# Eleven of block 2's 22 MLP pairs by seven half-size products, on two sets of banks, with TensorE in written order

## The chip, the cores and the metric

The kernel runs on one NeuronCore of a Trainium2 chip. Its engines work beside each other, each through its own queue of instructions in a fixed order: TensorE (PE, matrix products, with its weight loads shown as PEld), VectorE (DVE), ScalarE (ACT), GpSimd (POOL) and SyncE (SP, which starts the transfers). TensorE writes into PSUM banks, from which VectorE and ScalarE read. The metric is the time of one execution on the device in microseconds. "Columns" are the width of a product's right-hand side: 512 are a whole one, 256 a half one.

## The reference

Two transformer blocks, 512 tokens of width 1024, all in fp32. The change is in the MLP of the second block alone:

```python
u = rmsnorm_2(x, norm_ffn_w[l])
up, gate = jnp.split(u @ w_ffn_up[l], 2, axis=-1)      # 1024 x 5632; D_FF_2 = 2816 = 22 * 128
a = causal_dwconv_2(up, ffn_conv_w[l], ffn_conv_b[l])  # 3 taps over the tokens
x = x + (jax.nn.silu(a) * gate) @ w_ffn_down[l]
...
return rmsnorm_2(x, norm_final_w)
```

## The kernel before

**Products.** An fp32 product is made of three products of numbers split into a high and a low half (mm3, L461 to L463: high by high, high by low, low by high). Activations lie transposed, 128 channels by 512 tokens to a tile; hs is the list of split results of the MLP's pairs.

**Weights.** All weights come in one stream, in the order of weight_order(), as units of 512 KB (eight 128 by 128 blocks). prefetch loads a unit into one of four "raw" buffers, ScalarE casts it to the high half (whi, L258), VectorE subtracts for the low half (wlo, L260); there are five buffers each of whi and wlo. A cast into a whi buffer must wait until TensorE has made the last product with what was in it.

**Block 2's MLP.** The 22 column tiles of up, each with its column tile of gate, are the 22 pairs. hidden2(i) makes a pair: two times 8 x 3 products of 512 columns into one bank each, then its tail of small operations: zp = up times the norm's factor rb (VectorE, L1676), conv3 (a scaling on ScalarE, L1585, two taps on VectorE, L1587), silu (ScalarE, L1678), times gate (VectorE, L1679), split into halves (ScalarE L529, VectorE L530). They run as pairs 0 to 8, eight "downs" (24 products each with w_ffn_down, L1691), pairs 9 to 16, eight downs, pairs 17 to 21. The last six tiles of down stand in a "tail" that goes through the 512 tokens in two halves, with the final norm of each half: sums of squares by small products with ones (L1757, L1759).

**Pairs by seven.** Block 1's MLP (about 400 to 720 us) makes 14 of its 16 pairs another way, with pairg: the pair is taken as a 2 x 2 block matrix of weights times a 2 x 2 block matrix of activations (two k tiles by two token halves, four times), and by a scheme of Strassen's kind this takes seven half-size products in place of eight: 7 x 4 x 3 = 84 of 256 columns in place of 48 of 512. It needs sums of weight blocks (seven_steps: the sums s75, s6, s4 on VectorE, L297, L315, L318; the casts and low halves of three sets of 1024 columns and of the 512 columns of operand "b", L305 and L310) and sums of activation blocks (rights). The seven results collect in four banks. A copy c0 of the first (ScalarE, L380) and four additions on VectorE (L386 to L389) put them together in a tile q that holds up and gate.

**Banks.** There are two kinds, "mm" and "sm", of four each. A plain product takes the next "mm" bank in turn; an "mm" seven pair takes all four. The first bank of a seven pair is free for the next product once c0 is copied.

**Order.** defer(n, f) runs f after n more products have been written; the list scheduler then settles the order of each engine, but block 1's seven pairs run as written on TensorE.

Of the kernel before, what the change touches and what calls it, by code (L numbers as in the profile page):

```python
# [9 lines left out]
F32 = mybir.dt.float32  # L10
F32R = mybir.dt.float32r
I32 = mybir.dt.int32
U8 = mybir.dt.uint8
AF = mybir.ActivationFunctionType
ALU = mybir.AluOpType
# [3 lines left out]
T = 512  # L19
# [40 lines left out]
def weight_order():  # L60


    seq = []
    seven = set()

    def pair(name, n1, n2):
        assert len(seq) % 8 == 0
        seven.add(len(seq) // 8)
        for n, o in ((n1, 0), (n2, 1), (n1, 1), (n2, 0)):
            for k in range(o, 8, 2):  # L70
                seq.append((name, k, n))

    def cols(name, ns, ks):
        for n in ns:
            for k in ks:
                seq.append((name, k, n))

    def rows(name, ks, ns):
        for k in ks:
            for n in ns:  # L80
                seq.append((name, k, n))

    r8 = range(8)
    for lo in (12, 8, 16):
        cols("w_in", range(lo, lo + 4), r8)
    rows("w_in", r8, range(4, 8))
    cols("w_in", range(0, 4), r8)
    cols("w_in", range(20, 24), r8)
    cols("xa_wk", r8, r8)
    rows("xa_wv", r8, range(4))  # L90
    rows("xa_wv", r8, range(4, 8))
    cols("w_out", range(NWO), range(4))
    cols("w_out", range(NWO), range(4, 8))
    cols("w_out", range(NWO, 8), r8)
    cols("xa_wq", r8, r8)
    cols("xa_wo", range(4), range(6))
    cols("xa_wo", range(4), (6, 7))
    cols("xa_wo", range(4, 8), r8)
    for what, i, g in ffn_order():
        if what == 1 and i < NPLAIN:  # L100
            cols("ffn_w1", (2 * i, 2 * i + 1), r8)
        elif what == 1:
            pair("ffn_w1", 2 * i, 2 * i + 1)
        else:
            cols("ffn_w2", [i], range(8 * g, 8 * g + 8))

    cols("w_in_2", [28, 29, 24, 25, 26, 27], r8)
    for i in range(8):
        cols("w_in_2", [8 + i, 16 + i, i], r8)
    cols("w_in_2", [30], r8)  # L110
    cols("w_conv_out_2", r8, r8)
    cols("w_in_2", range(31, 38), r8)
    for i in range(8):
        cols("w_in_2", [38 + i], r8)
        cols("w_attn_out_2", [i], range(4))
    cols("w_mix_out_2", r8, r8)
    for g, (a, b) in enumerate(GROUPS2):
        for i in range(a + (1 if g else 0), b + (1 if b < 22 else 0)):
            cols("w_ffn_up_2", [i, 22 + i], r8)
        cols("w_ffn_down_2", r8, range(a, b))  # L120
    return seq, seven


def ffn_order():


    for i in range(4):
        yield 1, i, 0
    for g in range(4):
        for n in range(8):  # L130
            if g < 3 and n % 4 == 0:
                yield 1, 4 * g + 4 + n // 4, g + 1
            yield 2, n, g
        if g < 3:
            yield 1, 4 * g + 6, g + 1
            yield 1, 4 * g + 7, g + 1


GROUPS2 = [(0, 8), (8, 16), (16, 22)]


# [27 lines left out]
def _build(ctx, tc, nc, A, out, stage):  # L169
# [5 lines left out]
    V, S, G, PE = nc.vector, nc.scalar, nc.gpsimd, nc.tensor  # L175
    cnt = [0]

    def nm(s):
        cnt[0] += 1
        return f"{s}_{cnt[0]}"  # L180

    def t2(dt=F32, shape=(P, T)):
        return ap_.tile(list(shape), dt, tag="t2", bufs=NSLOT, name=nm("t2"))
# [36 lines left out]
    def col(name, i=0, n=1):  # L220
        o = COFF[name][0] + i
        return colt[:, o:o + n]
# [169 lines left out]
    def rights(x, gname, xs):  # L392


        H = T // 2
        f = lambda hl, j: (hl[0][:, j * H:(j + 1) * H], hl[1][:, j * H:(j + 1) * H])
        res = [{} for _ in range(len(xs) // 2)]
        steps = []

        def one(p):  # L400
            st = {}

            def s0():
                st["a"], st["b"] = t2(), t2()
                S.activation(st["a"], x[2 * p], AF.Copy, scale=col(gname, 2 * p))
                S.activation(st["b"], x[2 * p + 1], AF.Copy, scale=col(gname, 2 * p + 1))

            def s1():
                a, b = st["a"], st["b"]
                st["v"], st["w"] = v, w = t2(), t2()  # L410
                V.tensor_sub(v[:, H:], b[:, H:], a[:, H:])
                V.scalar_tensor_tensor(out=w[:, :H], in0=a[:, H:], scalar=1.0, in1=a[:, :H],
                                       op0=ALU.mult, op1=ALU.subtract)
                V.tensor_scalar_mul(v[:, :H], w[:, :H], -1.0)
                V.tensor_sub(w[:, :H], w[:, :H], b[:, H:])
                V.scalar_tensor_tensor(out=w[:, H:], in0=w[:, :H], scalar=-1.0, in1=b[:, :H],
                                       op0=ALU.mult, op1=ALU.subtract)

            def s2():
                vs = split(st["v"])  # L420
                ws = split(st["w"])
                res[p].update({"B11": f(xs[2 * p], 0), "B21": f(xs[2 * p + 1], 0), "B22": f(xs[2 * p + 1], 1),
                               "V1": f(vs, 0), "V7": f(vs, 1), "V6": f(ws, 0), "T4": f(ws, 1)})

            return [s0, s1, s2]

        for p in range(len(xs) // 2):
            steps.extend(one(p))
        return res, steps
# [3 lines left out]
    def defer(n, fn):  # L433

        late.append((wst["i"] + n, fn))
        late.sort(key=lambda e: e[0])
# [37 lines left out]
    def lin(name, n, ks, mv, ps=None, start=True, stop=True, off=0):  # L474
        if ps is None:
            ps = bank()
        for _ in ling(name, n, ks, mv, ps, start, stop, off):
            pass
        return ps
# [41 lines left out]
    def split(src, g=None, shape=(P, T)):  # L521

        hi, lo = t2(F32R, shape), t2(F32R, shape)
        split_to(hi, lo, src, g)
        return hi, lo
# [10 lines left out]
    def zpad():  # L536
        zp = ap_.tile([P, T + 4], F32, tag="t2", bufs=NSLOT, name=nm("zp"))
        G.memset(zp[:, 0:4], 0.0)
        return zp
# [71 lines left out]
    def wide_later(acc, eps, rbt, at, square):  # L611

        def part():
            hi, lo = split(acc)
            ps = bank("sm")
            PE.matmul(ps, lhsT=ones_r, rhs=hi, start=True, stop=False)
            PE.matmul(ps, lhsT=ones_r, rhs=lo, start=False, stop=True)
            if square:
                V.tensor_scalar(rbt, ps, 1.0 / D, eps, op0=ALU.mult, op1=ALU.add)
                V.reciprocal(rbt, rbt)  # L620
                return
            a = tmp()
            V.tensor_scalar(a, ps, 1.0 / D, eps, op0=ALU.mult, op1=ALU.add)
            step(rsqrt_g(rbt, a))

        def step(g):
            if next(g, None) is not None:
                defer(1, lambda: step(g))

        defer(at, part)  # L630

    def acc_tile():
        return ap_.tile([P, T], F32, tag="t2", bufs=NSLOT, name=nm("acc"))


    xs = []
# [4 lines left out]
    acc = acc_tile()  # L641
# [11 lines left out]
    rb = row_bc(rc, 4)  # L653
# [22 lines left out]
    kf, qf, vf, gv, gu, gate, ys = [], [], [], [], [], [], []  # L676
# [530 lines left out]
    acc = acc_tile()  # L1207
# [9 lines left out]
    xs = xs2  # L1217
# [77 lines left out]
    acc = acc_tile()  # L1295
# [8 lines left out]
    xs = xs2  # L1304
# [4 lines left out]
    rops, steps = rights(x, "norm_ffn", xs)  # L1309
# [68 lines left out]
    acc = acc_tile()  # L1378
# [23 lines left out]
    xs = xs2  # L1402

    rc12, rc, rb, rb1 = tinyc(8), tinyc(4), acc_tile(), acc_tile()
# [178 lines left out]
    def conv3(zp, wname, j):  # L1583
        c = tmp()
        S.activation(c, zp[:, 2:2 + T], AF.Copy, scale=col(wname, 3 * j))  # L1585
        for i in (1, 2):
            V.scalar_tensor_tensor(out=c, in0=zp[:, 2 + i:2 + i + T], scalar=col(wname, 3 * j + i),  # L1587
                                   in1=c, op0=ALU.mult, op1=ALU.add)
        return c
# [67 lines left out]
    acc = acc_tile()  # L1657
# [8 lines left out]
    xs = xs2  # L1666


    rb = acc_tile()
    wide_later(acc, 1e-5, rb, 3, False)  # L1670

    def hidden2(i):
        ps = lin("w_ffn_up_2", i, range(8), xs)
        psg = lin("w_ffn_up_2", 22 + i, range(8), xs)
        zp = zpad()
        V.tensor_mul(zp[:, 4:], ps, rb)  # L1676
        c = conv3(zp, "ffn_conv_w_2", i)
        S.activation(c, c, AF.Silu, bias=col("ffn_conv_b_2", i))  # L1678
        V.tensor_mul(c, c, psg)  # L1679
        return split(c)  # L1680

    hs = []
    for g, (a, b) in enumerate(GROUPS2):
        hs += [hidden2(i) for i in range(a + (1 if g else 0), b)]
# [10 lines left out]

    a, b = GROUPS2[2]
    nk = b - a
# [25 lines left out]
    for hf in range(2):  # L1723
        ts = slice(hf * H, (hf + 1) * H)
        acc = acc_tile()
        pss = [None] * 8
        ss = bank("sm")[:, :H]
        st = {}
# [140 lines left out]
```

## Time and profile before

| what | value |
|---|---|
| three runs | 1543.88, 1544.42 and 1546.13 us (median 1544.42) |
| profiled execution | 1543.86 us, its span 1542.1 us |
| mean granted TensorE clock | 0.997 |
| busy share of the span | PE 98%, DVE 65%, ACT 44%, POOL 9% |
| block 2's MLP without its tail | 1159 to 1493 us |

The span runs from the first to the last recorded instruction; some 1.8 us lie outside. Busy shares are means over stages with different limits. PE's busy time comes from modelled ends of pipelined products, so the start-to-start time of products is the better measure of what one costs.

### The profile page before, as it was taken

The numbers are of one execution on the slowest core, as the hardware profiler recorded it, in microseconds if no ns is written. First come the engines' busy times: TensorE is split into PE (matmuls) and PEld (weight loads), VectorE is DVE, ScalarE is ACT, GpSimd is POOL, SyncE is SP. The second block draws the span as 40 slices with busy tenths as digits, with TensorE's granted clock in tenths as the row PEclk, the third lists the DMA queues.
The fourth block names the chain that finished last, engine by engine and source line by source line (L and its number), as shares of the span: only waits on it lengthen the run. The fifth ranks groups of instructions, "written<-read, shape, count | busy, mean of one in ns | idle before, by whom it ended". The sixth has DMA issues, their size and how long they took to land.

```text
span 1542.1 us, 20324 instructions
## 1 busy us (share of the span) xinstructions
PE 1514.8 (98%) x7904; PEld 1274.9 (83%) x7904; DVE 999.0 (65%) x1623; ACT 674.9 (44%) x1117; POOL 143.5 (9%) x162
## 2 busy tenths in 40 slices
PE   8999999999999999999999999999999999999996
PEld 6888898888888888989888888888888888888886
DVE  6897675554786786767688767335546555555557
ACT  6666555443564353535444444333334331332233
POOL 0002120200201212011400000000020002001101
PEclk9999999999999999999999999999999999999998
DMA  6033335221223323324043222222232222232311
GB/s 254 20 111 100 112 130 197 96 68 55 82 72 106 96 95 109 104 83 137 14 150 131 83 82 83 81 92 92 92 96 96 96 96 96 96 96 92 100 41 56
DMA packets 51505, 149.89 MB, mean 97 GB/s; under 512 B 9552, under 2 KB 14032, under 8 KB 51408
## 3 DMA queue, kind: packets, MB, share of 16 engines
q1 hardware_dynamic: 51264, 148.32, 29.1%
q8 instruction: 62, 1.02, 0.3%
q14 instruction: 35, 0.29, 0.1%
q10 hardware_dynamic: 144, 0.26, 0.1%
HBM read 143.97 MB, written 3.28 MB: 95 GB/s over the span
## 4 chain that ended last, share of the span: by engine, by line
PE 95%; DVE 2%; ACT 2%; issue 1%; DMA 0%; POOL 0%; SPq 0%; DVEq 0%; ACTq 0%; POOLq 0%
PE mm L461 28%; PE mm L462 27%; PE mm L463 27%; PE sm L463 2%; PE sm L461 2%; PE sm L462 2%; ACT whi L258 0%; ACT t L1090 0%; DVE wlo L260 0%; DMA raw<-wts 0%; PE sm L581 0%; PE sm L1576 0%; PE sm L1575 0%; PE sm L1577 0%; PE sm L713 0%
## 5 line engine op out<-in xcount | busy, mean ns | idle before, releaser
L461 PE MATMUL mm<-t,whi 128*128 128x512 f32 (+1 forms) x1888 | 719.9, 381 | 9.1 <-ACT whi L254 7.3
L462 PE MATMUL mm<-t,whi 128*128 128x512 f32 (+1 forms) x1888 | 716.7, 380 | 0.2 <-DVE t L530 0.2
L463 PE MATMUL mm<-t,wlo 128*128 128x512 f32 (+1 forms) x1888 | 716.8, 380 | 0.0
L258 ACT CAST whi<-raw 128x1024 fp32r<-128x1024 f32 x226 | 236.5, 1051 | 432.7 <-PE mm L462 286.2
L461 PEld LDWEIGHTS mm<-t,whi 128*128 128x128 f32 x1888 | 355.3, 188 | 77.9 <-ACT whi L254 7.3
L463 PEld LDWEIGHTS mm<-t,wlo 128*128 128x128 f32 x1888 | 355.3, 188 | 72.1 <-DVE wlo L260 0.8
L462 PEld LDWEIGHTS mm<-t,whi 128*128 128x128 f32 x1888 | 355.2, 188 | 69.6 <-DVE t L530 0.4
L260 DVE TENSOR_TENSOR wlo<-raw,whi 128x1024 fp32r<-128x1024 f32 x219 | 287.4, 1312 | 81.8 <-ACT whi L258 78.8
L575 POOL TENSOR_TENSOR acc<-acc,tmp 128x512 f32<-128x512 f32 (+1 forms) x37 | 52.7, 1432 | 468.2 <-ACT tmp L571 467.9
L1436 DVE TENSOR_TENSOR tmp<-mm,acc 128x512 f32<-128x512 f32 x46 | 31.7, 689 | 48.8 <-PE mm L463 46.8
L1393 POOL TENSOR_TENSOR res<-res,tmp 128x512 f32<-128x512 f32 x24 | 39.0, 1638 | 247.9 <-DVE tmp L1391 217.3
L310 DVE TENSOR_TENSOR wlo<-sraw,whi 128x1024 fp32r<-128x1024 f32 x28 | 38.4, 1375 | 26.5 <-ACT whi L305 26.5
L461 PE MATMUL sm<-t,whi 128*128 128x256 f32 (+1 forms) x176 | 50.4, 286 | 1.8 <-ACT whi L305 1.8
L1676 DVE TENSOR_TENSOR zp<-mm,acc 128x512 f32<-128x512 f32 x22 | 15.2, 691 | 55.0 <-PE mm L463 54.9
L463 PE MATMUL sm<-t,wlo 128*128 128x256 f32 (+1 forms) x176 | 50.4, 286 | 0.0
L462 PE MATMUL sm<-t,whi 128*128 128x256 f32 (+1 forms) x176 | 50.2, 285 | 0.0
L305 ACT CAST whi<-sraw 128x1024 fp32r<-128x1024 f32 x28 | 29.3, 1047 | 45.8 <-PE mm L462 41.0
L1692 POOL TENSOR_TENSOR res<-res,tmp 128x512 f32<-128x512 f32 x16 | 20.7, 1294 | 260.2 <-DVE tmp L1691 260.2
L1679 DVE TENSOR_TENSOR tmp<-tmp,mm 128x512 f32<-128x512 f32 x22 | 15.1, 687 | 43.4 <-PE mm L463 42.6
L1391 DVE TENSOR_TENSOR tmp<-mm,acc 128x512 f32<-128x512 f32 x32 | 21.6, 686 | 26.5 <-PE mm L463 22.6
L1691 DVE TENSOR_TENSOR tmp<-mm,acc 128x512 f32<-128x512 f32 x16 | 11.1, 692 | 39.2 <-PE mm L463 39.2
L461 PEld LDWEIGHTS sm<-t,whi 128*128 128x128 f32 x176 | 33.1, 188 | 2.5 <-ACT whi L305 2.0
(379 smaller groups left out, 1840.2 us busy)
## 6 DMA issues: line engine op xcount, KB each, us to landing
raw<-wts SPq DMA_DIRECT2D x259, 512.0 KB, 3.7
res<-xT SPq DMA_DIRECT2D x16, 256.0 KB, 5.2
yT<-t SPq DMA_DIRECT2D x6, 256.0 KB, 2.3
tmp<-tmp SPq DMA_DIRECT2D x20, 64.0 KB, 2.0
gm<-gm SPq DMA_DIRECT2D x4, 256.0 KB, 5.2
dn<-ch SPq DMA_DIRECT2D x4, 256.0 KB, 2.3
tmp<-memT SPq DMA_DIRECT2D x4, 256.0 KB, 2.6
cst<-const SPq DMA_DIRECT2D x1, 576.0 KB, 6.7
```

The source lines that it names most:

```text
L258: S.copy(hi, r)
L260: defer(LO, lambda r=r, hi=hi, lo=lo: V.tensor_sub(lo, r, hi.bitcast(F32)))
L305: S.copy(t[n][0], s)
L310: V.tensor_sub(t[n][1], src(), t[n][0].bitcast(F32))
L461: PE.matmul(ps, lhsT=ahi, rhs=bhi, start=start, stop=False)
L462: PE.matmul(ps, lhsT=ahi, rhs=blo, start=False, stop=False)
L463: PE.matmul(ps, lhsT=alo, rhs=bhi, start=False, stop=stop)
L575: eng.tensor_add(acc[:, :w], acc[:, :w], dst[:, :w])
L1391: V.tensor_mul(t, ps, rb2)
L1393: G.tensor_add(x[n], x[n], t)
L1436: V.tensor_mul(t, ps, rb)
L1692: G.tensor_add(x[n], x[n], t)
```

## The change

Eleven pairs (SEVEN2) of block 2's MLP go through pairg: 5, 8, 11, 14, 17 and 20 on "sm" banks, 6, 9, 12, 15 and 18 on "mm" banks, which the plain pairs and the downs use too. Their weights stand in the stream as pairg wants them. The sums of activation blocks (rights) are made during the first pairs. From here on TensorE runs in written order, the tail too. A seven pair's tail is spread by defer over the products that follow. The sum for the norm's factor rb is put off from 3 to 8 k steps.

```diff
--- before.py
+++ after.py
@@ -116,7 +116,10 @@
     cols("w_mix_out_2", r8, r8)
     for g, (a, b) in enumerate(GROUPS2):
         for i in range(a + (1 if g else 0), b + (1 if b < 22 else 0)):
-            cols("w_ffn_up_2", [i, 22 + i], r8)
+            if i in SEVEN2:
+                pair("w_ffn_up_2", i, 22 + i)
+            else:
+                cols("w_ffn_up_2", [i, 22 + i], r8)
         cols("w_ffn_down_2", r8, range(a, b))
     return seq, seven
 
@@ -136,6 +139,8 @@
             yield 1, 4 * g + 7, g + 1
 
 
+
+SEVEN2 = {5, 6, 8, 9, 11, 12, 14, 15, 17, 18, 20}
 GROUPS2 = [(0, 8), (8, 16), (16, 22)]
 
 
@@ -1666,10 +1671,44 @@
     xs = xs2
 
 
+
+    ctx.enter_context(tc.manual_schedule(engines={mybir.EngineType.PE}))
     rb = acc_tile()
-    wide_later(acc, 1e-5, rb, 3, False)
+    wide_later(acc, 1e-5, rb, 8, False)
+
+    rops2, steps = rights(x, "norm_ffn_w_2", xs)
+    for j, f in enumerate(steps):
+        defer(10 + 14 * (j // 3) + 2 * (j % 3), f)
+
+    def hidden7(i):
+        hl = (t2(F32R), t2(F32R))
+
+        def then(q):
+            zp = zpad()
+            V.tensor_mul(zp[:, 4:], q[:, :T], rb)
+            st = {}
+
+            def taps():
+                st["c"] = conv3(zp, "ffn_conv_w_2", i)
+
+            def gate():
+                c = st["c"]
+                S.activation(c, c, AF.Silu, bias=col("ffn_conv_b_2", i))
+                defer(1, lambda: V.scalar_tensor_tensor(out=c, in0=q[:, T:], scalar=-1.0, in1=c,
+                                                        op0=ALU.mult, op1=ALU.mult))
+                defer(2, lambda: S.copy(hl[0], c))
+                defer(4, lambda: V.tensor_sub(hl[1], c, hl[0].bitcast(F32)))
+
+            defer(1, taps)
+            defer(2, gate)
+
+        for _ in pairg("w_ffn_up_2", i, 22 + i, rops2, then, "sm" if i % 3 == 2 else "mm"):
+            pass
+        return hl
 
     def hidden2(i):
+        if i in SEVEN2:
+            return hidden7(i)
         ps = lin("w_ffn_up_2", i, range(8), xs)
         psg = lin("w_ffn_up_2", 22 + i, range(8), xs)
         zp = zpad()
```

The program is the same row by row up to block 2's MLP. TensorE's rows go from 7448 to 7844, VectorE's from 1578 to 1705, ScalarE's from 964 to 1013; the transfers are the same in number.

ScalarE around pairs 11 and 12, before. The first and the second row are the scaling for the tap and the silu of pair 11, t_2173 is the cast of hs11, the next two the scaling and the silu of pair 12.

```order
L1585 ACTIVATE tmp_11643<-zp_11640,colt 128x512 [waits DVE_49,Pool_49]
L1678 ACTIVATE tmp_11643<-tmp_11643,colt 128x512 [waits DVE_49]
L258 CAST whi_11762<-raw_11685 128x1024 [waits DMAHW5_49,PE_49,Activation_49]
L529 CAST t_2173_11649<-tmp_11643 128x512 [waits DVE_49]
L258 CAST whi_11806<-raw_11729 128x1024 [waits DMAHW6_49,PE_49,Activation_49]
L1585 ACTIVATE tmp_11718<-zp_11715,colt 128x512 [waits DVE_49,Pool_49]
L1678 ACTIVATE tmp_11718<-tmp_11718,colt 128x512 [waits DVE_49]
```

ScalarE at the same place, after. tmp_12045 is pair 11, t_2243 the cast of hs11, t_2272 the copy c0 of pair 12 (whose first bank is mm_12038, the next that plain pair 13 needs); whi_12157, whi_12170 and whi_12191 are the casts of pair 14's weights.

```order
L310 CAST whi_12157<-raw_12034 128x1024 [waits DMAHW5_49,PE_49,Activation_49]
L310 CAST whi_12170<-sraw_12155 128x1024 [waits DVE_49,PE_49,Activation_49]
L1590 ACTIVATE tmp_12045<-zp_12029,colt 128x512 [waits DVE_49,Pool_49]
L310 CAST whi_12191<-sraw_12180 128x1024 [waits DVE_49,PE_49]
L1696 ACTIVATE tmp_12045<-tmp_12045,colt 128x512 [waits DVE_49]
L1699 CAST t_2243_11905<-tmp_12045 128x512 [waits DVE_49]
L385 COPY t_2272_12071<-mm_12038 128x256
```

VectorE at this place, after: wlo_12192 is the low half of the cast whi_12191, the two L1592 are the taps of pair 11, L1697 is its gate.

```order
L315 TENSOR_TENSOR wlo_12171<-sraw_12155,whi_12170 128x1024 [waits PE_49,Activation_49]
L1592 SCALAR_TENSOR_TENSOR tmp_12045<-zp_12029,colt,tmp_12045 128x512 [waits Activation_49]
L315 TENSOR_TENSOR wlo_12192<-sraw_12180,whi_12191 128x1024 [waits PE_49,Activation_49]
L1592 SCALAR_TENSOR_TENSOR tmp_12045<-zp_12029,colt,tmp_12045 128x512 [waits DVE_49]
L302 TENSOR_TENSOR sraw_12255<-raw_12206,raw_12248 128x1024 [waits DMAHW7_49,DMAHW0_49]
L1697 SCALAR_TENSOR_TENSOR tmp_12045<-q_12024,tmp_12045 128x512 [waits Activation_49]
```

Before, casts of weights and tails of pairs take turns and nothing on this queue frees a bank. Now three casts for a pair stand together, a tap stands behind the low half of the third, and the copy that frees a bank stands last.

ScalarE ahead of pair 5, the first seven pair, after: whi_10979 is the last of the pair's three casts, tmp_10849 and t_2069 are the tail of pair 3, t_2084 the cast of pair 5's operand b.

```order
L310 CAST whi_10979<-sraw_10960 128x1024 [waits PE_49,Activation_49]
L1590 ACTIVATE tmp_10849<-zp_10846,colt 128x512 [waits DVE_49,Pool_49]
L1717 ACTIVATE tmp_10849<-tmp_10849,colt 128x512 [waits DVE_49]
L534 CAST t_2069_10855<-tmp_10849 128x512 [waits DVE_49]
L310 CAST t_2084_10907<-raw_10860 128x512 [waits DMAHW4_49]
```

Before, there is no operand b; the cast of each unit stands a pair ahead. Now the cast of b is the last of five.

TensorE in the middle of the tail, before: sm_12676 collects the sums of squares of the first half, mm_12966 is the last product tile of the first half, mm_12991 the first of the second half.

```order
L463 MATMUL mm_12966<-t_2333_12671,wlo_12635 128x256
L461 MATMUL mm_12991<-t_2233_12024,whi_12634 128x256 [waits DVE_49]
L462 MATMUL mm_12991<-t_2234_12025,whi_12634 128x256
L1757 MATMUL sm_12676<-acc_12675,cst 128x256 [waits DVE_49,PE_49]
L463 MATMUL mm_12991<-t_2233_12024,wlo_12635 128x256
L461 MATMUL mm_12991<-t_2285_12371,whi_12634 128x256
L462 MATMUL mm_12991<-t_2286_12372,whi_12634 128x256
L1759 MATMUL sm_12676<-acc_12767,cst 128x256 [waits Activation_49]
L463 MATMUL mm_12991<-t_2285_12371,wlo_12635 128x256
```

The same place, after (sm_13392, mm_13624, mm_13682):

```order
L468 MATMUL mm_13624<-t_2475_13387,t_2518_13556 128x256
L1796 MATMUL sm_13392<-acc_13391,cst 128x256 [waits DVE_49]
L1798 MATMUL sm_13392<-acc_13483,cst 128x256 [waits Activation_49]
L466 MATMUL mm_13682<-t_2345_12566,whi_13350 128x256
L467 MATMUL mm_13682<-t_2346_12567,whi_13350 128x256
L468 MATMUL mm_13682<-t_2345_12566,wlo_13351 128x256
```

The small products stood two and five products into the second half; now they stand together, ahead of it.

## Rows read from the trace of the kernel before

**Rows 1.** The page: busy time, slices of the granted clock, chain that ended last.

```profile
PE 1514.8 (98%) x7904; PEld 1274.9 (83%) x7904; DVE 999.0 (65%) x1623; ACT 674.9 (44%) x1117; POOL 143.5 (9%) x162
...
PEclk9999999999999999999999999999999999999998
...
PE 95%; DVE 2%; ACT 2%; issue 1%; DMA 0%; POOL 0%; SPq 0%; DVEq 0%; ACTq 0%; POOLq 0%
```

**Rows 2.** Windows of block 2's MLP: pairs 0 to 7, downs, pairs 9 to 16.

```profile
1159.00:1245.00 86.00, 86.00 (x372) 69.34 (x371) 52.01 (x65) 34.05 (x42) 0.00 (x0) 1.00 0.28 92
...
1264.00:1308.00 44.00, 44.00 (x193) 35.71 (x191) 23.68 (x16) 8.43 (x8) 10.61 (x16) 1.00 0.27 89
1308.00:1398.00 90.00, 90.00 (x390) 72.98 (x389) 46.76 (x56) 32.35 (x40) 0.00 (x0) 1.00 0.31 99
```

**Rows 3.** Windows of one seven pair of block 1 and one plain pair of block 2.

```profile
619.09:629.00 9.91, 9.91 (x87) 9.91 (x86) 6.63 (x10) 6.58 (x10) 0.00 (x0) 1.00 0.17 55
1209.53:1220.64 11.11, 11.11 (x50) 9.01 (x49) 5.85 (x7) 4.03 (x5) 0.00 (x0) 1.00 0.30 96
```

**Rows 4.** TensorE's waits, 400 to 720 us (line, awaited: us in all, times, longest).

```profile
PE sm L461 <- ACT whi L305: 1.8, 1, 1.8
PE mm L461 <- ACT t L305: 1.5, 1, 1.5
PE mm L461 <- ACT t L380: 1.3, 2, 0.7
```

**Rows 5.** Timeline of 638.3 to 640 us: start, duration, instruction, [idle before, releaser].

```profile
638.37 1.04 ACT L258 CAST whi<-raw 128x1024 fp32r<-128x1024 f32 x1
...
638.78 0.28 PE L463 MATMUL mm<-t,wlo 128*128 128x256 f32 x1
639.32 0.36 ACT L380 COPY t<-mm 128x256 f32<-128x256 f32 x1
...
639.74 0.50 PE L461 MATMUL mm<-t,whi 128*128 128x512 f32 x1 [0.68 <-ACT t L380]
```

**Rows 6.** Timeline of 437 to 442 us.

```profile
440.45 0.61 ACT L305 CAST t<-raw 128x512 fp32r<-128x512 f32 x1
...
441.12 0.39 PE L461 MATMUL mm<-t,t 128*128 128x256 f32 x1 [1.54 <-ACT t L305]
```

**Rows 7.** VectorE's timeline of 639.8 to 655 us.

```profile
639.85 0.68 DVE L386 TENSOR_TENSOR q<-mm,t 128x512 f32<-128x512 f32 x1
640.45 1.22 DVE L260 TENSOR_TENSOR wlo<-raw,whi 128x1024 fp32r<-128x1024 f32 x1
641.58 0.68 DVE L387 TENSOR_TENSOR q<-mm,q 128x512 f32<-128x512 f32 x1
...
643.31 0.42 DVE L388 TENSOR_TENSOR q<-mm,q 128x256 f32<-128x256 f32 x1
```

**Rows 8.** Groups of instructions, 1159 to 1493 us (busy us, mean ns, idle before).

```profile
L1587 DVE SCALAR_TENSOR_TENSOR tmp<-zp,colt,tmp 128x512 f32<-128x512 f32 x44 | 32.9, 749 | 3.3 <-ACT tmp L1585 2.6
...
L1678 ACT ACTIVATE tmp<-tmp,colt 128x512 f32<-128x512 f32 x22 | 15.9, 724 | 41.0 <-DVE tmp L1587 41.0
...
L1679 DVE TENSOR_TENSOR tmp<-tmp,mm 128x512 f32<-128x512 f32 x21 | 14.4, 687 | 40.8 <-PE mm L463 40.1 <-ACT tmp L1678 0.8
...
L529 ACT CAST t<-tmp 128x512 fp32r<-128x512 f32 x21 | 13.1, 622 | 4.1 <-DVE tmp L1679 4.1
```

**Rows 9.** TensorE's timeline, in the middle of the tail.

```profile
1512.59 0.28 PE L462 MATMUL mm<-t,whi 128*128 128x256 f32 x1
...
1514.24 0.28 PE L461 MATMUL mm<-t,t 128*128 128x256 f32 x1
```

**Rows 10.** TensorE's timeline, at the end of the tail.

```profile
1528.34 0.28 PE L463 MATMUL mm<-t,t 128*128 128x256 f32 x1
1528.83 0.67 PE L1757 MATMUL sm<-acc,cst 128*128 128x256 f32 x2 [0.20 <-DVE acc L575]
1530.11 0.70 PE L1759 MATMUL sm<-acc,cst 128*128 128x256 f32 x2 [0.61 <-ACT acc L571]
```

## The prediction

> **What bounds the kernel now.** The first views to read are the page's busy times and its chain. TensorE is busy 98% of the span, the chain that ended last is TensorE for 95%, and the granted clock is at nine tenths or more of 2.4 GHz in every slice until the last [rows 1]. So time comes off only where TensorE does less, and goes on only where it is made to wait. The windows of block 2's MLP come next: from 1159 to 1245 (pairs) VectorE is busy 52.0 of 86 us and ScalarE 34.1, from 1308 to 1398 46.8 and 32.4 of 90 [rows 2]. TensorE is busy in every us of them, so block 2's MLP loses nothing today; each wait that the change brings is a loss.
>
> **What a pair by seven costs TensorE.** Block 1 already runs such pairs, so the trace has the price. Window by window, a seven pair (84 products of 256 columns) takes 9.92 us, a plain pair (48 of 512 columns) 11.12 [rows 3]. That saves 1.20 us a pair, for eleven pairs **13.2 us**, as long as nothing waits. The additions of the right-hand sides (20 on VectorE, 8 scalings and 8 splits) come early in the MLP, with a third of VectorE free, and I cost them at nothing beyond the entries below. The weight traffic is the same.
>
> The Trainium skill, "TensorE: Matmul & The Clock Gate", section on the back-to-back issue gap, gives a sustained gap of 81 ns at 128 columns and 131 at 512; on a straight line between (an estimate) 256 cost 98 ns, and a seven pair would take 8.2 us against 6.3 for a plain one, 1.9 more. The rows show 118 and 231.5 ns a product, so the trace decides, and it is against that figure.
>
> **What a pair by seven costs the others.** VectorE gets, per seven pair, four operations of 1024 columns (three low halves and one sum of weights, 1.22 each), six of 512 (two sums, b's low half, three of q, 0.68 each) and one of 0.42, together 9.4, and then block 2's own tail of a pair, zp, two taps of 0.75, gate and low half of 0.69, 3.6 [rows 7, 8]. From start to start each takes some 0.08 less (a low half begun at 640.45 is followed at 641.58 [rows 7]), so 16 of them are 11.7 to 12.2 us, against 5.85 in a plain pair [rows 3]. Two sevens and a plain pair are up to 30.3 us of VectorE against 2 x 9.92 + 11.12 = 30.96 of TensorE: VectorE is nearly full from pair 8 to 16, and just behind at pairs 17 to 20. Only the downs, where it is busy 23.7 of 44 us [rows 2], give it air.
>
> **Where TensorE will wait.** Block 1's stretch tells which waits a seven pair brings: for the cast of its weights and of operand b (1.8 and 1.5 us, at the first pairs of a run), and for the copy of c0 (0.7 and 0.6), because a plain product needs the bank that the copy frees [rows 4]. With some tenths that the view does not list, 6.5 us by the spacing of products over 14 pairs. The copy's case is at 638: a cast begun at 638.37 holds ScalarE, the copy runs at 639.32 and the plain product starts at 639.74, 0.84 late [rows 5]. In block 2 every one of five "mm" sevens is followed by something on the same banks. I followed each such copy and cast up the new order of ScalarE and VectorE (each takes its rows in turn):
>
> - *Pair 5, the first seven.* Operand b's cast t_2084 stands behind the tap, silu and cast of pair 3, and those behind the cast whi_10979, whose buffer pair 4's last product frees. After the end of pair 4, one behind the other: that cast 1.05, its low half (which stands ahead of pair 3's taps on VectorE) 1.23, taps 1.5, silu 0.72, gate 0.69, cast 0.62, cast of b 0.62, together 6.4 [rows 5, 7, 8]. b is needed 24 products of 118 ns, 2.83 us, into the pair. That is at least 3.6, and with hand-overs and what VectorE has left of pair 2 I take 4.3 us. Block 1's like wait, where the cast started late at 440.45 and the product at 441.12, was 1.5 to 1.7 [rows 6].
> - *Pair 7, plain after the "mm" seven 6.* c0's copy stands behind a cast that needs the end of pair 6 (1.05) and behind the cast of hs5 (0.62), which needs pair 5's gate; with the copy, 0.36, at least 2.05, and with the gate 3.0 us.
> - *Pair 13, plain after the "mm" seven 12.* The copy of c0 (t_2272) stands in ScalarE's queue behind the cast of hs11, that behind pair 11's gate, silu and second tap; the second tap stands on VectorE behind wlo_12192, and that waits for whi_12191, the fifth cast after one that pair 12's last product still reads. After the end of pair 12 therefore all in a row: cast 1.05, low half 1.23, tap 0.75, silu 0.72, gate 0.75, cast 0.62, copy 0.36 [rows 5, 7, 8] = 5.5, with hand-overs and the sum of pair 15's weights between, 6.2 us. Before, the same queue has at this place only casts that wait for their own buffers, and nothing on TensorE waits for those.
> - *Pairs 16 and 19, after 15 and 18.* The copy stands behind one cast that ends late, as at 638 in block 1: 0.65 each. Pair 10: none, its copy stands early.
> - *Pairs 4 and 12:* 0.3 each, for zp and gate, and for b's low half.
>
> Sum 15.4; with about 0.1 for each restart (the first product after a wait took 0.39 or 0.50 for 0.28 or 0.40 [rows 5, 6]) 16.0.
>
> **The tail.** In written order the two small sums of the first half (L1796, L1798) stand directly behind the products of the last of the first half; before, they stood 2 and 5 products further on. The second half's, which always stood so, show what that is: its last product begins at 1528.34, the small sums at 1528.83 and 1530.11, the second pair waiting for ScalarE [rows 10]; from the end of the product (0.12 later) to that of the four (two spacings of some 0.2 after 1530.11) that is 2.1 us. In the middle, from 1512.59 to 1514.24, the four take 1.65 less five products of 0.118, 1.06 us [rows 9]. So 1.0 more. Pair 21's gate and low half, in a queue that is behind, come 0.9 later before the tail's splits: 0.9. The tail costs 1.9.
>
> **Sum.** 1543.86 (the profiled execution; its span is 1542.1) - 13.2 + 16.0 + 1.9 = 1548.56, **1548.5**. The median of the runs is 1544.42, 0.56 above the profiled one; I do not add it, and the range holds it. Bounds: with the least waits (3.6, 2.05, 5.5, 0.65 twice, none at 4 and 12, and the tail's 1.9) 14.4 are lost, which gives 1545.0; with block 1's whole rate (6.5/14 a pair, 5.1 in all, and the tail's 1.9) it is 1537.7.
>
> **Rivals.**
> A, the forecast: the queues run as read, waits of 14 to 20 us exceed the gain; 1545 to 1551.
> B, on the other side: pair 11's tail is done before pair 12 ends. It decides whether the second tap is issued before wlo_12192 gets its cast; then pair 13 waits 0.65 like pairs 16 and 19, 5.5 less, and the time is 1543.0. If pair 5 also waits only block 1's 1.7, it is 1540.4; at block 1's rate everywhere 1537.7. For it: block 1 shows this rate with the same queues. Against: block 1's tail of a pair is two VectorE operations behind one cast, block 2's a chain of four hand-overs, and the rows of ScalarE stand in the order told above. The Trainium skill, "Perfetto Trace Analysis", on matmuls, says to rotate independent groups of products through different banks so that evacuation overlaps them; the change does this with two sets, by which rule no product would wait. Rows 4 show two such waits with the same rotation in block 1.
> C: VectorE itself bounds the runs of sevens: from pair 8 to 20 each pair adds some tenths to a backlog that the downs do not absorb, 3 to 4 us over A: 1552.
> D: products of 256 columns are dearer here than in block 1. At 132 ns (11.12 / 84) a seven pair saves nothing, and with the waits of A the time is 1561.8. Rows 3 speak against it: 118 ns in the same loop.
>
> **Chances.** A 0.62, B 0.27 (two thirds near 1543, a third at 1537.7 to 1541.3), C 0.09, D 0.02. A measurement of this kernel can tell 0.2%, 3.1 us, from no change: slower is over 1547.5, faster under 1541.3. Of A two thirds lie above 1547.5 (its own range is 1545 to 1551), the rest within; C and D above. Slower 0.53 (0.42 of A, C and D), within 0.38 (0.20 of A, 0.18 of B), faster 0.09. The range 1542.0 to 1552.0 leaves out the fast third of B and most of D, and takes in the least and the largest sum of A.
>
> **What the profile will show.** TensorE's busy time down by about 13, its waits in the MLP from none to some 15 us. Its list of waits: the largest for c0's copy (L385), among them one of 5 to 6 us at pair 13 and one of 2 to 3 at pair 7; one of about 4 for a cast (L310) 2.8 us into pair 5. VectorE above 85% busy from pair 8 to 16. In the tail a wait of about 1 us for L1798 in the middle of it. Wrong would be the forecast if the list has no wait over 2 us (then B), if the waits are for VectorE's q operations in each pair (then C), or if a seven pair without a wait takes other than 9.9 us (then D).

## The result, and the profile after

The changed kernel takes 1558.59 us (median of 4 runs, 1556.36 to 1559.27) against 1544.15 before: 14.4 us, a ratio of 1.0089 with a 95% interval of 1.0077 to 1.0101. Slower was forecast, but by 4 us; the time lies 6.6 us above the range. The profiled execution took 1559.27 us (span 1557.5), 15.41 more than the one before.

The page's busy times, and the granted clock in 40 slices:

```profile
PE 1513.7 (97%) x8300; PEld 1293.0 (83%) x8300; DVE 1078.8 (69%) x1750; ACT 704.3 (45%) x1166; POOL 144.4 (9%) x162
...
PEclk9999999999999999999999999999999999999998
```

Against [rows 1] TensorE is busy about as long as before, although it should do 13 us less: the busy time also grows where the clock is low (in the fastest run below, with the same products and no such waits, it is 1501.5). So the next view is TensorE's waits (engine, line, awaited: us in all, times, longest) in block 2's MLP and its tail, where before there was none ahead of the tail:

```profile
PE mm L466 <- ACT t L385: 9.9, 4, 6.0
PE sm L466 <- ACT t L310: 3.5, 1, 3.5
PE sm L1796 <- DVE acc L580: 2.1, 1, 2.1
PE sm L1798 <- ACT acc L576: 0.8, 1, 0.8
PE mm L466 <- ACT t L534: 0.6, 1, 0.6
```

The copy c0 (L385) is awaited four times, once for 6.0 us; operand b's cast (L310) once for 3.5; in the tail the small sums wait for VectorE. The timeline shows the longest, at the end of pair 12 (TensorE's small products between are left out):

```profile
1352.58 1.05 ACT L310 CAST whi<-sraw 128x1024 fp32r<-128x1024 f32 x1 [1.78 <-PE mm L467]
...
1353.66 1.23 DVE L315 TENSOR_TENSOR wlo<-sraw,whi 128x1024 fp32r<-128x1024 f32 x1 [0.41 <-ACT whi L310]
...
1354.16 1.03 ACT L310 CAST whi<-sraw 128x1024 fp32r<-128x1024 f32 x1
...
1355.47 1.22 DVE L315 TENSOR_TENSOR wlo<-sraw,whi 128x1024 fp32r<-128x1024 f32 x1
1356.60 0.74 DVE L1592 SCALAR_TENSOR_TENSOR tmp<-zp,colt,tmp 128x512 f32<-128x512 f32 x1
...
1357.38 0.72 ACT L1696 ACTIVATE tmp<-tmp,colt 128x512 f32<-128x512 f32 x1 [2.20 <-DVE tmp L1592]
1358.40 0.68 DVE L1697 SCALAR_TENSOR_TENSOR tmp<-q,tmp 128x512 f32<-128x512 f32 x1
...
1359.12 0.62 ACT L1699 CAST t<-tmp 128x512 fp32r<-128x512 f32 x1 [1.01 <-DVE tmp L1697]
1359.64 0.36 ACT L385 COPY t<-mm 128x256 f32<-128x256 f32 x1
...
1360.06 0.79 PE L466 MATMUL mm<-t,whi 128*128 128x512 f32 x1 [6.03 <-ACT t L385]
```

This is the chain that the prediction wrote down for pair 13, instruction by instruction: the cast at 1354.16 when pair 12's last product is done, its low half, the second tap, silu, gate, the cast of hs11, the copy, the product. VectorE and ScalarE take their rows strictly in turn; the Trainium skill, "TensorE: Matmul & The Clock Gate", under the architectural detail of the array, says that these two queues are strict FIFO, and this timeline agrees: ScalarE does nothing from 1355.2 to 1357.4, with a copy behind it whose input, pair 12's first product, had been finished for some 10 us. VectorE is busy all through this wait, so the timeline alone does not tell a copy that stands in the wrong place from a VectorE that is full; the runs on c0 below do.

What had not been in the prediction shows in the windows (start and end, length, the busy times of TensorE, its weight loads, VectorE, ScalarE and GpSimd with their instructions, then the granted clock as a share of 2.4 GHz):

```profile
1223.50:1228.00 4.50, 4.12 (x19) 3.92 (x20) 2.93 (x5) 1.37 (x3) 0.10 (x1) 0.62 0.34 119
1245.40:1248.50 3.10, 3.06 (x7) 2.44 (x8) 3.00 (x6) 0.00 (x0) 0.00 (x0) 0.52 0.00 0
1353.90:1360.00 6.10, 0.13 (x2) 0.00 (x0) 6.07 (x8) 2.89 (x5) 0.00 (x0) 0.80 0.13 50
1360.00:1364.30 4.30, 4.24 (x10) 3.37 (x11) 4.11 (x7) 0.01 (x1) 0.00 (x0) 0.50 0.02 4
1364.30:1393.00 28.70, 28.70 (x206) 26.97 (x206) 19.83 (x26) 14.08 (x19) 0.20 (x2) 1.00 0.30 96
1470.60:1474.00 3.40, 3.40 (x15) 2.79 (x16) 3.37 (x6) 0.79 (x1) 0.00 (x0) 1.00 0.28 108
1524.60:1528.30 3.70, 3.56 (x15) 3.22 (x15) 2.00 (x5) 0.65 (x2) 0.00 (x0) 0.54 0.00 0
```

From 1360.0 to 1364.3, behind the 6.2 us wait, the granted clock is 0.50, the 1.2 GHz level, and then 1.00 again. The same holds behind pair 5's wait (0.62 over a window that includes its end), pair 7's (0.52) and the tail's (0.54), but not behind pair 19's 1.2 us.

**Account.** A product without a wait starts 231.7 ns (512 columns) or 117.7 ns (256) after the one before it. What the start-to-start times have beyond that is put down to its place; a wait here takes in the slow first product or two behind it:

| where | forecast, us | measured, us |
|---|---|---|
| eleven shorter pairs | -13.2 | -12.7 (9.93 to 9.97 a pair without a wait, plain 11.10 to 11.13) |
| wait at pairs 4, 5, 7 | 0.3, 4.3, 3.0 | 0.3, 4.4, 3.0 |
| wait at pairs 12, 13 | 0.3, 6.2 | 0.4, 6.6 |
| wait at pairs 16, 19, 20 | 0.65, 0.65, 0 | 0.7, 1.3, 0.3 |
| restarts | 0.6 | in the waits |
| products at the lower clock, block 2's pairs | 0 | 4.25 |
| tail | 1.9 | 5.4 |
| ahead of block 2's MLP | 0 | 1.8 |

The measured waits of the pairs are 16.9 (0.2 of them were there before); -12.7 + 16.7 + 4.25 + 5.4 + 1.8 = 15.4, the difference of the two profiles.

### The profile page after: what moved, and what is told of

It reads as the page before. It is cut to its first block, busy times and chain, and to the rows that moved or that the text cites. A ratio compares the mean times of both kernels' runs of the same rounds, so it can differ in the third digit from the quotient of the medians.

```text
span 1557.5 us, 21300 instructions
## 1 busy us (share of the span) xinstructions
PE 1513.7 (97%) x8300; PEld 1293.0 (83%) x8300; DVE 1078.8 (69%) x1750; ACT 704.3 (45%) x1166; POOL 144.4 (9%) x162
## 5 line engine op out<-in xcount | busy, mean ns | idle before, releaser
L466 PE MATMUL mm<-t,whi 128*128 128x512 f32 (+1 forms) x1832 | 688.3, 376 | 18.6 <-ACT t L385 11.2
L467 PE MATMUL mm<-t,whi 128*128 128x512 f32 (+1 forms) x1832 | 683.9, 374 | 0.2 <-DVE t L535 0.2
L468 PE MATMUL mm<-t,wlo 128*128 128x512 f32 (+1 forms) x1832 | 683.3, 373 | 0.0
L265 DVE TENSOR_TENSOR wlo<-raw,whi 128x1024 fp32r<-128x1024 f32 x190 | 237.0, 1247 | 78.7 <-ACT whi L263 78.1
L315 DVE TENSOR_TENSOR wlo<-sraw,whi 128x1024 fp32r<-128x1024 f32 x50 | 70.5, 1411 | 34.9 <-ACT whi L310 34.4
L466 PE MATMUL sm<-t,whi 128*128 128x256 f32 (+1 forms) x320 | 91.1, 285 | 1.8 <-ACT whi L310 1.8
L310 ACT CAST whi<-sraw 128x1024 fp32r<-128x1024 f32 x50 | 52.4, 1048 | 88.2 <-PE mm L467 72.5
L467 PE MATMUL sm<-t,whi 128*128 128x256 f32 (+1 forms) x320 | 91.0, 284 | 0.0
L468 PE MATMUL sm<-t,wlo 128*128 128x256 f32 (+1 forms) x320 | 91.0, 284 | 0.0
L1441 DVE TENSOR_TENSOR tmp<-mm,acc 128x512 f32<-128x512 f32 x46 | 31.7, 689 | 48.8 <-PE mm L468 46.8
L466 PEld LDWEIGHTS sm<-t,whi 128*128 128x128 f32 x320 | 60.6, 189 | 2.8 <-ACT whi L310 2.0
L467 PEld LDWEIGHTS sm<-t,whi 128*128 128x128 f32 x320 | 60.6, 189 | 0.7
L468 PEld LDWEIGHTS sm<-t,wlo 128*128 128x128 f32 x320 | 60.6, 189 | 0.4
L310 ACT CAST whi<-raw 128x1024 fp32r<-128x1024 f32 x25 | 26.2, 1050 | 51.3 <-PE mm L467 42.9
L466 PE MATMUL sm<-t,t 128*128 128x256 f32 (+1 forms) x132 | 39.4, 299 | 3.5 <-ACT t L310 3.5
```

The source lines that it names most:

```text
L265: defer(LO, lambda r=r, hi=hi, lo=lo: V.tensor_sub(lo, r, hi.bitcast(F32)))
L310: S.copy(t[n][0], s)
L315: V.tensor_sub(t[n][1], src(), t[n][0].bitcast(F32))
L466: PE.matmul(ps, lhsT=ahi, rhs=bhi, start=start, stop=False)
L467: PE.matmul(ps, lhsT=ahi, rhs=blo, start=False, stop=False)
L468: PE.matmul(ps, lhsT=alo, rhs=bhi, start=False, stop=stop)
```

## The experiments

Each was timed beside the kernel before on its chip; the ratios are to that kernel.

**Only the written order.**

```diff
-SEVEN2 = {5, 6, 8, 9, 11, 12, 14, 15, 17, 18, 20}
+SEVEN2 = set()
```

> No pair of block 2 goes by seven; the written order of TensorE, the sums of the right-hand sides and the later sum for rb stay (the sums are made and not used). Theory (the loss lies in waits that the sevens bring, the clock that falls behind them, and a tail in which VectorE is late): no wait in the pairs and downs, the clock at full level there, and in the tail only the small sums' 1.0 us: 1544.2 + 1 = 1545, from 1544 to 1547. Rival (the written order itself costs, since products can no longer be moved past a wait): several us of waits among the pairs, and over 1550.

Measured: 1550.16 us, 1.0034 [1.0021, 1.0046]. All of TensorE's waits from 1150 us to the end of its work are:

```profile
PE sm L1796 <- DVE acc L580: 2.2, 1, 2.2
PE sm L1798 <- ACT acc L576: 0.8, 1, 0.8
```

None lies among the pairs, so the theory holds there and the rival falls; but the tail costs 3.9 us (from the last whole product to the last of all 41.6 us, before 37.7), not 1.0. In the two profiles another 2.7 lie ahead of block 2's MLP: 1.2 at the start of the kernel, and 1.5 by the lower clock behind a wait in block 1 (below). The expected time was missed because the tail's price was.

**The sevens in the scheduler's order.**

```diff
-    ctx.enter_context(tc.manual_schedule(engines={mybir.EngineType.PE}))
```

> All eleven sevens, TensorE in the scheduler's order again. Theory: the waits for c0's copy and for operand b come from ScalarE's queue and stay where no other product can be put ahead; the tail's 5.5 us mostly go, since the small sums move behind later products: 1552 to 1556. Rival (the written order forces the waits): plain products are put ahead of the blocked ones, waits and fallen clock go, and the time is 1558.6 - 26 = near 1533 to 1540.

Measured: 1548.19 us, 1.0022 [1.0013, 1.0032]: below the theory's 1552 to 1556 and above the rival's 1533 to 1540, so neither had the size. The waits are shorter, not gone; the two largest entries:

```profile
PE mm L466 <- ACT t L385: 6.9, 4, 2.4
PE mm L466 <- DVE tmp L1717: 1.5, 1, 1.5
```

The longest for the copy is 2.4 instead of 6.0, since the scheduler puts products of another tile ahead (36 of pair 14's ahead of pair 13). So part of the loss was the written order's, in the pairs too; the waits' origin is not.

**A buffer of its own for c0, in block 2.**

```diff
-                c0 = t2()[:, :H]
+                c0 = (wp.tile([P, H], F32, tag="c0", bufs=1, name=nm("c0"))
+                      if name == "w_ffn_up_2" else t2()[:, :H])
```

> In block 2 the copy c0 gets a buffer of its own instead of one of the 67 shared slots; with that it stands in ScalarE's queue ahead of the casts and tails that it stood behind (pair 12's copy now right behind operand b's cast). Theory (the waits at pairs 7, 13, 16 and 19 are that queue's order, and the order came from a slot that was free only late): 10.6 us of waits and some 3.4 of fallen clock behind pairs 7 and 13 go: 1558.6 - 14 = 1544.6, from 1542 to 1548, with pair 5's wait and the tail as they were. Rival (VectorE is full from pair 8 on, and bounds the pairs in any case): waits for VectorE's operations on the banks take their place, and the time stays over 1553.

Measured: 1545.03 us, 0.9998 [0.9989, 1.0007]: 13.6 us less than the changed kernel, from one copy's place in a queue. The waits left:

```profile
PE sm L467 <- ACT t L310: 3.9, 1, 3.9
PE sm L1797 <- DVE acc L581: 2.1, 1, 2.1
...
PE sm L469 <- DVE t L315: 0.7, 2, 0.4
```

None is for the copy, and among the pairs VectorE's are 0.7 in all: pairs 7, 13, 16 and 19 waited for ScalarE's order, and VectorE did not bound them.

**Only the six sevens on the second set.**

```diff
-SEVEN2 = {5, 6, 8, 9, 11, 12, 14, 15, 17, 18, 20}
+SEVEN2 = {5, 8, 11, 14, 17, 20}
```

> Only the six sevens on the second set of banks (5, 8, 11, 14, 17, 20); the five on the first set are plain again. Theory: the gain is 6 x 1.20 = 7.2 us, no c0 wait is left, pair 5 keeps its wait for operand b with the fallen clock behind it (some 6 us), the tail costs 1 to 4: 1544.2 - 7.2 + 8 = 1545, from 1542 to 1548. Rival (any seven pair in block 2 brings its own waits, in equal shares): 6/11 of 14.4 us, 1552.

Measured: 1542.95 us, 0.9994 [0.9985, 1.0003]. No wait for a copy; pair 5's is 1.3 us here and the clock stays up behind it, so the time lies below the 1545 expected. A seven pair does not cost a fixed share: it depends on what follows on its banks.

**The tail in the scheduler's order again**, on top of c0's buffer:

```diff
-    ctx.enter_context(tc.manual_schedule(engines={mybir.EngineType.PE}))
+    written = tc.manual_schedule(engines={mybir.EngineType.PE})
+    written.__enter__()
...
+    written.__exit__(None, None, None)
     a, b = GROUPS2[2]
```

> As the run with the copy's own buffer (1545.0), but the written order of TensorE ends ahead of the tail; the scheduler puts the two small sums 20 and 23 products into the second half again, where they stood before the change. Theory (the small sums wait because the 20 products that covered VectorE's way to them now stand behind them, and the clock falls in that wait): 2.3 us of wait, 1.0 of gaps and 1.4 of fallen clock go but for 0.7: 1541.0, from 1539.5 to 1542.5. Rival (VectorE comes late because pair 21's tail and the splits are late): the wait moves behind the tile ahead of the sums, and the time stays over 1544.

Measured: 1539.48 us, 0.9966 [0.9954, 0.9979]: 5.5 less. The two profiles differ by 5.8: 4.3 in the tail (42.1 to 37.9 us from the last whole product to the last of all) and 1.6 by the clock in block 1, which fell in the one and not in the other.

**A buffer of its own for operand b**, on top of c0's buffer, and 65 shared slots instead of 67:

```diff
-                t[n] = (wd(F32R, "whi", NWS), wd(F32R, "wlo", NWS)) if w > T else (t2(F32R), t2(F32R))
+                t[n] = ((wd(F32R, "whi", NWS), wd(F32R, "wlo", NWS)) if w > T else
+                        tuple(wp.tile([P, T], F32R, tag=g, bufs=1, name=nm(g)) for g in ("bh", "bl")))
```

> As the run with the copy's own buffer (1545.0), and operand b's two halves get a buffer each of their own, paid for with two of the 67 shared slots; pair 5's cast of b then stands 22 places further ahead in ScalarE's queue. Theory (that cast stood late for want of a free slot while the sums of the right-hand sides held theirs): pair 5's 4.1 us of wait, its 0.9 behind it and 1.25 of fallen clock go: 1539.0, from 1537 to 1542. Rival (pair 5 waits for the cast of its third weights, or VectorE's low half of b, as much): over 1543. With two slots fewer, other tiles may come late: up to 3 us against it.

Measured: 1533.42 us, 0.9926 [0.9914, 0.9939]. Pair 5 does not wait at all. The saving is 11.6, not 6.0. The two profiles differ by 11.2: 8.2 in block 2's MLP, since b's low halves (awaited 0.7) and the last pairs are no longer late either, 2.0 in block 1 and 1.0 ahead of it. Block 1 has the same operand and loses its wait of 1.5 for b [rows 4, 6]; the clock also stays up there (1.5), as it does in other profiles without the buffer, and its copies are awaited longer (2.0 for 1.3).

**Both together.**

> Both of the last two together. If the causes are separate, their savings add: 1545.0 - 4.0 - 6.0 = 1535, from 1533 to 1538. That is 13.2 us of shorter pairs less some 4 of restarts and small waits, against 1544.4 before. Rival (freed from these waits, TensorE runs into VectorE, which is full from pair 8 to 20): over 1540, with new waits for q's additions or low halves.

Measured: 1529.97 us, 0.9904 [0.9889, 0.9919]. The savings add (3.5 for the tail here; 4.4 in the two profiles), and the one new wait for VectorE is of 0.3 us.

**Block 1's copies too**, on top of both:

```diff
-                c0 = (wp.tile([P, H], F32, tag="c0", bufs=1, name=nm("c0"))
-                      if name == "w_ffn_up_2" else t2()[:, :H])
+                c0 = wp.tile([P, H], F32, tag="c0", bufs=1, name=nm("c0"))
```

> As the run before it, and block 1's seven pairs too take the copy's own buffer. Theory: the two waits of 0.8 us in block 1 for that copy have the same cause (no free slot) and go: 1533.5, from 1531 to 1537. Rival (in block 1 the copy is late because its queue is busy): no difference from the run before it.

Measured: 1525.18 us, 0.9873 [0.9860, 0.9887]: the fastest, 19 us under the kernel before. It lies 4.8 under the run before it, where 1.5 were expected, since not only the waits for the two copies but the 1.8 for a cast of weights went as well; the rest of the miss is that run's. The first four entries of its list of waits over the whole kernel, and VectorE's share in pairs 9 to 16:

```profile
PE mm L467 <- ACT whi L259: 6.2, 1, 6.2
PE sm L899 <- DVE tiny L552: 1.5, 1, 1.5
PE mm L467 <- DVE tiny L561: 0.5, 1, 0.5
PE sm L1801 <- ACT acc L577: 0.5, 1, 0.5
```

```profile
1296.50:1379.50 83.00, 83.00 (x556) 76.25 (x555) 70.13 (x92) 39.99 (x51) 0.26 (x4) 1.00 0.32 109
```

None lies among the pairs of either block, with VectorE busy 70.1 of 83 us (84%).

**The right-hand sides earlier**, on top of c0's buffer and the free tail, b in shared slots:

```diff
-        defer(10 + 14 * (j // 3) + 2 * (j % 3), f)
+        defer(6 + 10 * (j // 3) + 2 * (j % 3), f)
```

> As the run with the copy's own buffer and the tail in the scheduler's order (1539.5), and the sums of the right-hand sides start after 6 products' steps instead of 10 and are spread over 10 a group instead of 14; operand b keeps shared slots. In ScalarE's queue pair 3's tail then stands ahead of the cast of pair 5's third weights, and b's cast right behind that cast. Theory (pair 5 waits for what stands ahead of b's cast, not for b's buffer): 1.05 + 0.62 us after pair 4's end are inside the 2.83 in which b is not needed, so the wait of 4.0, 0.7 behind it and 1.3 of fallen clock go: 1533.5, from 1532 to 1536. Rival (it was the buffer of b): no change, 1539.5.

Measured: 1538.77 us, 0.9959 [0.9947, 0.9972], nearly as without it. By the time alone the rival would be right, but the trace says otherwise. Pair 5 no longer waits for b's cast; the one wait of over half a microsecond in block 2 up to the tail is this, 25 us earlier:

```profile
PE mm L467 <- DVE zp L1717: 4.1, 1, 4.1
```

VectorE, with the same sums in fewer pairs, makes zp 4.1 us late, and 2.5 us of lower clock follow; just ahead of zp in its queue stand a low half that waits 1.1 us for ScalarE's cast, and two halves of the sums. So pair 5's wait was what stood ahead of b's cast, and the sums, which the prediction costed at nothing, are free only where they stood.

**The changed kernel with the tail freed alone.**

> The changed kernel with one edit: the written order of TensorE ends ahead of the tail. Theory: the waits of the pairs stay (pair 13 some 6 us, pair 5 some 4, pair 7 some 2.6); the small sums' 2.3 us, the gaps and the fallen clock of the tail go: 1558.6 - 4.5 = 1554, from 1552 to 1555.5. Rival (with pair 21's end late, VectorE's lag moves elsewhere in the tail): over 1556.5.

Measured: 1553.77 us, 1.0058 [1.0045, 1.0070]. The waits of the pairs are what they were (9.9 and 3.5).

**The changed kernel with 65 slots.**

> The changed kernel with 65 shared slots instead of 67, nothing else. In ScalarE's queue every copy c0 and every cast of b stays in its place. Theory (the places come from the order in which the program asks for shared tiles, not from a lack of free ones): the same time, 1557 to 1560. Rival (the shared slots are full, and that is what made the copies late): later copies and over 1561.

Measured: 1557.97 us, 1.0084 [1.0070, 1.0098]. A lack of free slots is not why the copies stood late; nor did the two slots given up in the runs with b's own buffer cost anything that shows.

**The changed kernel with the copy written one product sooner.**

```diff
-            if j == 1:
+            if j == 0:
                 c0 = t2()[:, :H]
```

> The changed kernel with one edit: the copy c0 is written one of the seven products sooner, right behind the product that it copies, in its shared slot as before. In ScalarE's queue pair 12's copy then stands ahead of the cast whi of pair 14's third weights and ahead of pair 11's silu and cast; pair 6's likewise. Theory (the waits are the queue's order alone): the waits at pairs 7, 13, 16 and 19 go with the fallen clock behind two of them, as with the copy's own buffer: 1545, from 1542.5 to 1548. Rival (the own buffer helped in another way, by freeing slots): waits at 7 and 13 stay, over 1555.

Measured: 1542.91 us, 0.9987 [0.9978, 0.9996]: 15.7 us less than the changed kernel for one digit, with the shared slot as before. The two profiles differ by 17.3: 10.4 in block 2's MLP (3 less than with the copy's own buffer), 5.7 ahead of it and the rest in the tail. Of the 5.7 most are the waits of block 1, whose copies the edit moves too, which the expectation had left out, and some 1.5 the clock behind one of them. The waits of block 2:

```profile
PE sm L466 <- ACT t L310: 4.7, 2, 3.5
PE sm L1796 <- DVE acc L580: 2.1, 1, 2.1
...
PE mm L466 <- ACT t L385: 0.5, 1, 0.5
```

One copy is still awaited, 0.5 us; b's cast is awaited at pair 5 as before and now, for 1.2, at pair 14; the tail's wait is as it was. With this run and the one on slots the cause is the place in ScalarE's queue, not the memory.

## Why the prediction was wrong

**What held.** The price of a seven pair from block 1 (12.7 gained for 13.2). The waits of the pairs, the large ones each at its place and for the named instruction: 16.9, slow first products included, for 15.4 and 0.6 of restarts; only pair 19's is twice its size. Rival B is refuted by the timeline of pair 12; D by 9.93 to 9.97 us a pair.

**Where the 10.7 us between 1548.56 and the profiled 1559.27 lie.** The clock behind the waits 4.25, the tail 3.5, ahead of the change 1.8, the waits 0.7, the shorter pairs 0.5. The direction was right for the reason given; the size was not, and two steps failed.

**The clock behind a wait was put at nothing.** The one term for what follows a wait, "with about 0.1 for each restart", was read off waits of 0.8 and 1.5 us. Behind the longer ones here the granted clock falls to 1.2 GHz and the products run at half speed for a while, which costs 1.4 us behind pair 5's wait, 1.1 behind pair 7's and 1.7 behind pair 13's, 4.25 in all, and 1.0 more in the tail. The prediction forecast three waits over 2 us and put no price on the clock; the trace of before, with no such wait inside a run of products, had none to show beyond the one of 2.0 us in block 1. The Trainium skill, "TensorE: Matmul & The Clock Gate", Part 1, says that an idle TensorE goes to the half-rate clock; the windows agree (0.50, 0.52, 0.54), and the sentence should have been weighed.

**The tail failed.** "They stood 2 and 5 products further on" is a misreading, and so are the words on mm_12966 ahead of the prediction. mm_12966 is not the last tile of the first half but the first of the second; VectorE's rows of the kernel before show it, where its sum goes into res_2832, the tile that the first half had begun with, behind the norm's first step:

```
L1753 TENSOR_TENSOR res_2846<-res_2846,tmp_12927 128x256
L1765 TENSOR_SCALAR tmp_12934<-sm_12676 128x256
...
L1752 TENSOR_TENSOR tmp_12985<-mm_12966,acc_10461 128x256
...
L1753 TENSOR_TENSOR res_2832<-res_2832,tmp_12985 128x256
```

That tile has 18 products, and the small sums stood 2 and 5 products behind it: they lost the cover of 20 and 23 products, 2.4 to 2.7 us. The changed kernel's timeline shows what that covered:

```profile
1522.95 0.42 DVE L1791 TENSOR_TENSOR tmp<-mm,acc 128x256 f32<-128x256 f32 x1
...
1523.58 0.43 DVE L580 TENSOR_TENSOR acc<-acc,tmp 128x256 f32<-128x256 f32 x1 [0.21 <-ACT tmp L576]
...
1524.06 0.70 PE L1796 MATMUL sm<-acc,cst 128*128 128x256 f32 x2 [2.10 <-DVE acc L580]
...
1524.90 1.22 PE L1798 MATMUL sm<-acc,cst 128*128 128x256 f32 x2
```

VectorE's last addition to acc ends at 1524.0, the sums had been due at 1521.8, and the clock falls behind that wait. The prediction had looked for 1 us at L1798; it was 2.1 at L1796, for VectorE. The price by the end of the kernel [rows 10], where the wait is for ScalarE alone, was the wrong pattern: in the middle VectorE is behind, with splits of weights in its queue that do not stand at the end (that it is these which make it late was not tried). Of 1.9 forecast it became 5.4; the tail alone, without a seven, costs 3.9, and in the scheduler's order it took 4.3 to 4.5 less in three pairs of profiles.

**1.8 us ahead of the change** come from the same instructions: 0.3 at the start of the kernel, and 1.5 because behind the same wait of 2.0 us in block 1 the clock stayed up in the profile before and fell in the one after (below). As far as the runs show this is chance and belongs to neither kernel.

**A term without effect.** VectorE's 11.7 to 12.2 us per seven pair were too many: 70.1 us in pairs 9 to 16 (five sevens, three plain of 5.85) make 10.5, and it is busy 84% there, not above 85%. C, that VectorE would bound the runs of sevens, is refuted by the run without waits; only where the sums of the right-hand sides are crowded does its queue hold TensorE.

**What stays open.** Why the scheduler places a copy or a cast late when its tile comes from the shared tag: a buffer of its own, or writing it one product earlier, moves it; two slots fewer do not. And by what chain block 1's wait for a cast of weights (1.8 [rows 4]) went in the two runs that moved the copies there: it was not followed.

## What to carry to other kernels

When a change makes one engine's queue free the banks of another, write down what stands ahead of the freeing instruction and when each of those gets its input: here that list gave the waits as 15.4 us, 16.0 with the restarts, where 16.9 were measured, and showed the cure, an edit of one digit. Price a wait of TensorE with the time at the lower clock behind it, not only with the wait. And before saying how far an instruction has moved, name the loop step of every tile between its two places.

## What the runs showed of the hardware

The clock behind a wait. Behind the same 2.0 us wait in block 1, in the same instructions, first the kernel before and then the changed one:

```profile
469.50:473.50 4.00, 3.92 (x18) 3.26 (x19) 4.00 (x6) 0.29 (x2) 0.00 (x0) 1.00 0.41 125
```

```profile
469.80:473.50 3.70, 3.56 (x10) 2.90 (x11) 3.70 (x6) 0.35 (x2) 0.00 (x0) 0.55 0.20 53
```

1.00 in the one, 0.55 in the other; of the twelve profiles that have this wait it fell in four, at a price of about 1.5 us, half the spread of the runs of one kernel (1542.48 to 1545.59 for the run with c0's buffer). In block 2, over all profiles, it fell behind every wait of 2.26 to 6.2 us (by the spacing of products) and behind none of up to 2.0; each fall cost some 1 to 3 us.
